# Two seven-product unit pairs moved from the fourth and sixth to the second and fourth place of an up panel pair

## The chip, the cores and the metric

The kernel runs on one core of a Trainium2 chip, as one launch. The metric is the device time of one execution in microseconds. A core has a matrix engine (TensorE, in the profile PE, with its weight loads as PEld), a vector engine (VectorE, DVE), a scalar engine (ScalarE, ACT), GpSimd (POOL) and SyncE (SP). The engines run their own instruction streams in order and wait for each other through semaphores. In this kernel SP issues the loads of the weights; ACT issues the transfers that turn tiles through DRAM.

## What is computed

Two layers of a decoder trunk on 256 tokens of width 2048 in float32: a gated linear attention layer and a forgetting attention layer, each with attention into 256 memory tokens, and each followed by a gated channel mixer. The change touches the first product of the mixer, `h @ w_up`:

```python
def conv_ffn(h, w_up, conv_w, conv_b, w_down):       # w_up: 2048 x 11264, w_down: 5632 x 2048
    u = causal_dwconv(h @ w_up, conv_w, conv_b)      # width 3, along the tokens
    a, val = split_cols(u, [FFN_HIDDEN, FFN_HIDDEN])
    return (jax.nn.silu(a) * val) @ w_down
```

## The kernel before

**Products in three parts.** A float32 product is made of three matmuls in a rounded format (float32r): the operands are cut into a high and a low part, and high x high, low x high and high x low are added in PSUM. The activations `h` are cut once (`split`). The weights are cut as they arrive: a unit of 128 x 1024 is loaded into `raw` (five buffers), ACT casts it to `whi`, and VectorE subtracts to get `wlo` (four buffers each). In `split_unit` these are lines 210, 211 and 220.

**Panels and units.** A weight panel of 512 columns and 2048 rows is eight units (`count` = 8), each with two chunks of 128 rows. `proj_tm` goes through one panel, `proj_two` through two with the activations of both 128-token halves. For the mixer, the 5632 hidden columns are worked through in three parts (`PARTS`: 16, 16 and 12 blocks of 128). An up panel holds two blocks of the gate and the same two of the value. Part one has eight up panels: two by `proj_two`, then two panel pairs by `seven_evacuated`, then two by `proj_tm`. Part two has three panel pairs and two single panels, part three two and two. After the up panels of a part come its four down panels. That makes seven panel pairs for each layer, and fourteen in all.

**Seven products in place of eight.** `proj_seven` takes two panels at once. For each of the eight places `u` there is a unit of the one and a unit of the other panel, a unit pair. At most places it makes the usual 24 matmuls (2 panels x 2 token halves x 2 chunks x 3 parts). At the places in `forms` it takes the 2 x 2 blocks of weights and tokens and makes seven block products in place of eight (21 matmuls). It pays for that with sums: `t13` and `t24` are sums of weight blocks (four VectorE subtractions of 128 x 512, lines 349 to 352), and these are cut as well (`halves`, lines 317 and 318: three of 128 x 1024 and one of 128 x 512, against two of 128 x 1024 at a plain place). The sums of the activations are made once for each mixer into the `mixed` tiles. Of the seven products three add straight into accumulators `acc`, and four have PSUM banks of their own (`m1`, `m5`, `m6`, `m7`; tiles `ps_t`, `ps_s` and `ps_o`). After the last place in `forms` the function `more` of `seven_evacuated` adds these up (lines 384 to 388) into the buffers of `t13` and `t24`, of which there is one each. There they stay, as `extra`, until the panels are evacuated after the eighth place: ACT scales an accumulator into `scaled` (line 1172), VectorE adds `extra` (line 1174) and transposes (line 442). The down panels (`add_seven`) use the same function with places three and five, or three, five and seven, counted from zero; their `more` (lines 1055 to 1062) runs after the last place.

**What sets the order.** The instructions are written out in program order, and a planner reorders them by priority and by its own simulated times. The loads and cuts of the weights get a priority as though they stood 300 instructions earlier (`AHEAD`), the subtractions for `t13` and `t24` 340. The order on each engine is fixed when the kernel is built. Other steps hang on a counter: `later((n, step))` runs a step after `n` more calls of `passed`, and every unit pair calls it twice, so a panel pair counts sixteen. An up panel writes its transposed tile at count 3, reads it back at 6, and is convolved at 8 to 11 (its partner at 10 to 13), in units of the panels that follow. The two sums for `mixed` are called at counts 18 and 20 from the mixer's start. Sixteen counts belong to `proj_two`, so both fall into the first panel pair.

Of the kernel before, what the change touches and what calls it, by code (L numbers as in the profile page):

```python
# [38 lines left out]
AHEAD = 300  # L39
SEVEN = ((3, 5), (3, 5, 7))  # L40
LAST = ()
UP = (3, 5)

SPREAD = [128 * q + 32 * k + i for k in range(4) for i in range(32) for q in range(4)]

# [95 lines left out]
def _trunk(ctx: ExitStack, tc: tile.TileContext, xt, xtok, memt, wp, wgu, gns, gfin, cnv, par, msk, out):  # L141
# [39 lines left out]
    def later(*steps):  # L181

        for units, step in steps:
            due.append([units, step])
# [190 lines left out]
    def seven_evacuated(keys, src, forms, evacs, tiles):  # L375

        n = where[keys[0]][0][2]
        extra = {}

        def more(m1, m5, m6, m7):  # L380
            p, q = (tiles(t, F32) for t in ("t13", "t24"))
            u, v, w = p[:, :n], p[:, n : 2 * n], q[:, :n]
            m1, m5, m6, m7 = (m[:, :n] for m in (m1, m5, m6, m7))
            S.activation(u, m1, AF.Copy)
            V.tensor_tensor(u, u, m6, ALU.add)
            V.tensor_tensor(v, u, m5, ALU.add)
            V.tensor_tensor(u, u, m7, ALU.add)
            V.tensor_tensor(w, u, m5, ALU.add)
            extra.update({(0, 0): m1, (1, 0): v, (0, 1): u, (1, 1): w})

        def evac(i):
            return lambda b, a: evacs[i](b, a, extra[i, b])

        proj_seven(keys, src, forms, [evac(i) for i in range(2)], tiles, more, True)

    def sums_of(src, chunks, f, h, form):

        for c, k in enumerate(chunks):
            V.tensor_tensor(h[:, c, :], *(src[k][:, i, :].bitcast(F32) for i in range(2)), ALU.add)
        (a0, a1), (b0, b1) = ([h[:, c, b * P : (b + 1) * P] for b in range(2)] for c in range(2))  # L400
        token_sums(a0, a1, b0, b1, f, form)
# [665 lines left out]
    def ffn(l, nx, h, m, then, ending=None):  # L1067
        with tc.tile_pool(name=f"ffn{l}", bufs=1) as fp, ExitStack() as ends:
# [16 lines left out]
            def form(t):  # L1085
                return lambda i: [t[:, k, i, :] for k in range(2)]

            mixed = [sp.tile([P, 2, 4, P], F32R, name=f"mixed{i}") for i in range(len(UP))]

            def mixed_at(u, t):  # L1090
                def step():
                    f, g = (tp.tile([P, 512], F32, name=n, tag="scaled", bufs=2) for n in ("sf", "sh"))
                    sums_of(h, (2 * u, 2 * u + 1), f.rearrange("p (i t) -> p i t", t=P),
                            g.rearrange("p (c t) -> p c t", t=T), [t[:, k, :, :] for k in range(2)])

                return step

            later(*[(18 + 2 * i, mixed_at(u, t)) for i, (u, t) in enumerate(zip(UP, mixed))])

            def taps(t, u, j, n, c):  # L1100

# [63 lines left out]
            def panel(j, base, slack=0):  # L1165
                held = []

                def evac(b, a, extra=None):
                    if not held:
                        held.append(Turn("turned"))  # L1170
                    e = tp.tile([P, 512], F32, name="scaled", tag="scaled", bufs=2)
                    S.activation(e, a, AF.Copy, scale=nx.col()[:, b : b + 1])
                    if extra is not None:
                        V.scalar_tensor_tensor(e, extra, nx.col()[:, b : b + 1], e, ALU.mult, ALU.add)
                    held[0].put(b, e)
                    if not b:
                        return
                    u = us[turn[0] % 2]
                    turn[0] += 1
                    later((3, held[0].write), (6, lambda: held[0].read(lambda k: u[:, k, 2:])))  # L1180
                    convolved(j, base, u, 8 + slack, j + 2 in (p[1] for p in PARTS))

                return evac

            parts = {lo: dict(zip(SEVEN[1] if p < len(PARTS) - 1 else LAST, tiles)) for p, (lo, _) in enumerate(PARTS)}
            for p, (lo, hi) in enumerate(PARTS):
# [5 lines left out]
                while len(js) > 2:  # L1192
                    seven_evacuated([("up", l, j) for j in js[:2]], h, {u: form(t) for u, t in zip(UP, mixed)},
                                    [panel(js[0], lo), panel(js[1], lo, 2)], spare_tile)
# [42 lines left out]
    memory[0].close()  # L1237
    n2, then, turns = preparing("kv", bufB)
    ffn(0, n, bufB, bufA, then)
    n, then, _ = preparing("ffn1", bufA)  # L1240
    fox(n2, turns, then)
# [40 lines left out]
    def closing(ends):  # L1282
        op = ends.enter_context(tc.tile_pool(name="store", bufs=1))
        made["y"] = op.tile([P, 2, 512], F32, name="y")
        return op

    ffn(1, n, bufA, bufB, None, (opened, closing))


# [83 lines left out]
```

## Time and profile before

| | |
|---|---|
| median of 3 runs | 2232.72 us (2230.32 to 2238.43) |
| the profiled execution | 2234.48 us, of which the span from the first to the last instruction is 2232.7 us |
| granted TensorE clock | 0.998 |
| busy | PE 2214.0 us, DVE 1808.7, ACT 1448.6, POOL 44.7 |
| read from HBM | 470.44 MB |

The page of the profile gives the busy time of each engine, the chain of work that ended last, and groups of instructions by line of the kernel. A row such as `wlo<-raw,whi` names what an instruction writes and reads. In a timeline, the bracket at the end of a row is the idle time of that engine ahead of the instruction, and what ended it. Up panel pairs of the first layer lie at about 508 to 594, 721 to 853 and 980 to 1065 us of the span, those of the second at about 1553 to 1638, 1767 to 1898 and 2024 to 2111.

### The profile page before, as it was taken

The page shows a single profiled execution, that of the slowest core. Times are in us where ns is not written, and L with a number is a line of the kernel's source. Part 1 is how long each engine was busy: PE and PEld are TensorE (multiplying, and loading weights), DVE is VectorE, ACT ScalarE, POOL GpSimd, SP SyncE. Part 2 cuts the span into 40 slices and gives each one's busy share as a digit, 9 for nine tenths or more (in the row PEclk, how much of TensorE's full clock was granted, in tenths as well). Part 3 has the DMA queues.
Part 4 walks back from the last instruction along what each step waited for, and adds up shares of the span by engine and source line. Part 5 has one row for each costly group of instructions (what it writes and reads, how often), then busy time and mean ns, then how long its engine had stood idle before and what let it go on. Part 6 is the DMA issues. An engine that isn't in the chain of part 4 may idle for free.

```text
span 2232.7 us, 29804 instructions
## 1 busy us (share of the span) xinstructions
PE 2214.0 (99%) x10183; PEld 1846.8 (83%) x10183; DVE 1808.7 (81%) x2650; ACT 1448.6 (65%) x2261; POOL 44.7 (2%) x71
## 2 busy tenths in 40 slices
PE   9999999999999999999999999999999999999998
PEld 7888888888888878888888898888888887888876
DVE  8568987669999898998877875666989989898876
ACT  7555666557785588657866555555877567855774
POOL 0000000000000000000000000000000000000000
PEclk9999999999999999999999999999999999999999
DMA  9875667677876678667878777668776667766684
GB/s 346 272 234 187 210 204 225 204 238 231 258 235 208 228 225 257 220 203 234 262 245 277 249 224 232 195 224 262 235 248 232 198 226 227 262 217 206 228 252 144
DMA packets 276896, 517.00 MB, mean 232 GB/s; under 512 B 149884, under 2 KB 158600, under 8 KB 276616
## 3 DMA queue, kind: packets, MB, share of 16 engines
q1 hardware_dynamic: 124296, 427.24, 57.7%
q10 hardware_dynamic: 149760, 80.51, 12.5%
q0 software_dynamic: 2688, 7.34, 1.2%
q8 instruction: 80, 1.31, 0.2%
q14 instruction: 72, 0.59, 0.1%
HBM read 470.44 MB, written 44.58 MB: 231 GB/s over the span
## 4 chain that ended last, share of the span: by engine, by line
PE 92%; DVE 2%; ACT 2%; DMA 2%; issue 1%; ACTq 0%; SPq 0%; DVEq 0%
PE acc L294 36%; PE acc L232 16%; PE acc L233 16%; PE acc L236 16%; PE ps_s L294 3%; PE ps_o L294 2%; PE ps_t L294 1%; DMA raw<-wp 1%; DMA turned<-square 1%; DVE wlo L220 1%; ACT whi L211 1%; ACT back L1109 1%; PE ps_s L837 0%; DVE wlo L318 0%; ACT back L1107 0%
## 5 line engine op out<-in xcount | busy, mean ns | idle before, releaser
L220 DVE TENSOR_TENSOR wlo<-raw,whi 128x1024 fp32r<-128x1024 f32 (+4 forms) x707 | 839.7, 1195 | 260.9 <-ACT whi L211 220.0
L211 ACT ACTIVATE whi<-raw 128x1024 fp32r<-128x1024 f32 (+4 forms) x707 | 725.2, 1035 | 427.6 <-PE acc L233 204.9
L232 PE MATMUL acc<-whi,B 128*128 128x512 f32 (+3 forms) x992 | 373.6, 381 | 1.3 <-ACT whi L211 1.3
L233 PE MATMUL acc<-whi,B 128*128 128x512 f32 (+3 forms) x992 | 373.3, 379 | 0.0
L294 PE MATMUL acc<-whi,B 128*128 128x512 f32 x1236 | 324.7, 392 | 2.1 <-ACT whi L211 2.1
L294 PE MATMUL acc<-whi,A 128*128 128x512 f32 x1224 | 321.6, 390 | 2.9 <-ACT whi L211 2.9
L294 PEld LDWEIGHTS acc<-whi,B 128*128 128x128 f32 x1236 | 232.8, 189 | 52.2 <-ACT whi L211 2.7
L294 PEld LDWEIGHTS acc<-whi,A 128*128 128x128 f32 x1224 | 229.5, 188 | 52.6 <-ACT whi L211 4.0
L232 PE MATMUL acc<-whi,A 128*128 128x512 f32 x672 | 261.3, 394 | 0.3 <-ACT whi L211 0.2
L233 PE MATMUL acc<-whi,A 128*128 128x512 f32 x672 | 260.3, 391 | 0.0
L236 PE MATMUL acc<-wlo,B 128*128 128x512 f32 (+3 forms) x992 | 257.0, 377 | 0.0
L232 PEld LDWEIGHTS acc<-whi,B 128*128 128x128 f32 x992 | 186.2, 188 | 31.1 <-ACT whi L211 1.7
L233 PEld LDWEIGHTS acc<-whi,B 128*128 128x128 f32 x992 | 186.0, 188 | 29.1 <-DVE B L528 0.4
L236 PEld LDWEIGHTS acc<-wlo,B 128*128 128x128 f32 x992 | 183.7, 188 | 28.7
L236 PE MATMUL acc<-wlo,A 128*128 128x512 f32 x672 | 182.2, 390 | 0.0
L294 PE MATMUL acc<-wlo,B 128*128 128x512 f32 x618 | 174.4, 390 | 0.0
L294 PE MATMUL acc<-wlo,A 128*128 128x512 f32 x612 | 173.6, 390 | 0.0
L318 DVE TENSOR_TENSOR wlo<-t,whi 128x1024 fp32r<-128x1024 f32 x102 | 123.8, 1221 | 35.1 <-ACT whi L317 27.8
L317 ACT ACTIVATE whi<-t 128x1024 fp32r<-128x1024 f32 x102 | 106.8, 1054 | 66.3 <-PE acc L294 44.2
L232 PEld LDWEIGHTS acc<-whi,A 128*128 128x128 f32 x672 | 126.2, 188 | 27.9 <-ACT whi L211 0.9
L233 PEld LDWEIGHTS acc<-whi,A 128*128 128x128 f32 x672 | 126.3, 188 | 26.1 <-DVE A L531 0.2
L236 PEld LDWEIGHTS acc<-wlo,A 128*128 128x128 f32 x672 | 126.0, 188 | 26.4 <-DVE wlo L220 0.3
(278 smaller groups left out, 2594.4 us busy)
## 6 DMA issues: line engine op xcount, KB each, us to landing
raw<-wp SPq DMA_DIRECT2D x743, 512.0 KB, 4.4
turned<-square ACTq DMA_DIRECT2D x61, 512.0 KB, 4.5
u<-turned ACTq DMA_DIRECT2D x176, 128.0 KB, 4.4
raw<-wp SPq DMA_DIRECT2D x32, 384.0 KB, 3.2
raw<-wp SPq DMA_DIRECT2D x24, 388.0 KB, 5.3
xturned<-square ACTq DMA_DIRECT2D x12, 512.0 KB, 4.2
back<-xturned ACTq DMA_DIRECT2D x40, 128.0 KB, 5.1
raw<-wp SPq DMA_DIRECT2D x8, 400.0 KB, 3.3
```

The costliest lines, as they stand in the source:

```text
L211: casts.append(S.activation(hi[:, s], raw[:, s], AF.Copy))
L220: V.tensor_tensor(lo[:, s], raw[:, s], hi[:, s].bitcast(F32), ALU.subtract)
L232: TE.matmul(acc[:, :n], xh, hi[:, s], start=first and j == 0, stop=False)
L233: TE.matmul(acc[:, :n], xl, hi[:, s], start=False, stop=False)
L236: TE.matmul(a, xh, ls, start=False, stop=stop)
L294: TE.matmul(a[:, :n], x, w, start=k not in begun, stop=calls[k] == 0)
L317: casts.append(S.activation(hi, raw, AF.Copy))
L318: V.tensor_tensor(lo, raw, hi.bitcast(F32), ALU.subtract)
L1109: S.activation(t[:, k, :], u[:, k, n : T + n], AF.Copy, scale=g[n])
```

## The change

The two places in `UP`, counted from zero, become 1 and 3 in place of 3 and 5. The weights are taken in the same order as before, and the number of instructions of each kind in a panel pair is the same. As the activation sums belong to the chunks of these places, they are now made of chunks 2, 3, 6 and 7 (before: 6, 7, 10 and 11), and the steps that make them are called at counts 10 and 12, which is within `proj_two`.

```diff
-UP = (3, 5)
+UP = (1, 3)
...
-            later(*[(18 + 2 * i, mixed_at(u, t)) for i, (u, t) in enumerate(zip(UP, mixed))])
+            later(*[(10 + 2 * i, mixed_at(u, t)) for i, (u, t) in enumerate(zip(UP, mixed))])
```

## The prediction

> **What bounds the kernel now.** I read the page first (engine totals, then the chain that ended last), then the windows cut at the fourteen pairs of up panels that the edit touches, then the timelines of VectorE (DVE), ScalarE (ACT) and TensorE (PE) around the two windows that stood out.
>
> ```profile
> PE 2214.0 (99%) x10183; PEld 1846.8 (83%) x10183; DVE 1808.7 (81%) x2650; ACT 1448.6 (65%) x2261; POOL 44.7 (2%) x71
> ...
> PE 92%; DVE 2%; ACT 2%; DMA 2%; issue 1%; ACTq 0%; SPq 0%; DVEq 0%
> ```
>
> TensorE sets the time: 2214.0 of 2232.7 us busy and 92% of the chain. The edit keeps every matmul, so it can only move the 18.7 us in which PE is idle, and what a stall costs in clock. The windows show how little of that lies in the fourteen pairs (columns: length, busy time of PE, PEld, DVE, ACT and POOL, granted clock, DMA share, GB/s).
>
> ```profile
> 720.60:763.00 42.40, 42.40 (x187) 34.92 (x186) 36.96 (x43) 22.60 (x25) 0.00 (x0) 1.00 0.66 215
> 763.00:805.30 42.30, 42.30 (x187) 34.84 (x187) 37.16 (x45) 33.10 (x52) 0.00 (x0) 1.00 0.70 228
> 805.30:853.00 47.70, 45.60 (x193) 36.83 (x192) 44.05 (x54) 35.95 (x57) 0.00 (x0) 0.96 0.75 237
> 1851.00:1898.00 47.00, 44.07 (x192) 35.67 (x191) 41.81 (x51) 34.43 (x56) 0.00 (x0) 1.00 0.73 229
> sum 607.00, PE 601.83 PEld 493.80 DVE 544.06 ACT 432.11 POOL 0.00; mean PE 42.99 PEld 35.27 DVE 38.86 ACT 30.86 POOL 0.00
> ```
>
> A pair takes some 42.3 us, PE all of it, except in two windows, one for each layer: the third pair of the middle part. Over all fourteen PE idles 607.00 - 601.83 = 5.17 us, of which 2.10 and 2.93 lie there; the clock of 0.96 costs the first another 0.04 x 47.7 = 1.9 us. So 7.1 us is all that the touched code could give back.
>
> What makes those two stalls: VectorE, cut into quarters of the pair before the first of them.
>
> ```profile
> 763.00:773.60 10.60, 10.60 (x48) 8.77 (x48) 10.60 (x15) 5.69 (x8) 0.00 (x0) 1.00 0.56 187
> 773.60:784.20 10.60, 10.60 (x49) 8.74 (x48) 5.46 (x7) 6.76 (x11) 0.00 (x0) 1.00 0.84 293
> 784.20:794.80 10.60, 10.60 (x48) 8.71 (x47) 10.60 (x13) 10.21 (x17) 0.00 (x0) 1.00 0.75 213
> 794.80:805.40 10.60, 10.60 (x49) 8.68 (x48) 10.60 (x13) 10.43 (x18) 0.00 (x0) 1.00 0.65 220
> ```
>
> VectorE is full while it evacuates the pair before (first quarter), half idle in the second, then full to the end, where both seven-product pairs, the convolution and the sums `more` fall together. What that leads to, from the chain (two rows), ACT (three) and PE (one):
>
> ```profile
> 807.78 1.15 DVE wlo L220
> ...
> 808.94 4.59 DMA raw<-wp
> ...
> 809.55 0.76 ACT L527 ACTIVATE A<-back 128x256 fp32r<-128x256 f32 x2 [0.73 <-DVE back L1139]
> 813.55 0.63 ACT L317 ACTIVATE vhi<-raw 128x512 fp32r<-128x512 f32 x1 [3.25 <-DMA raw<-wp]
> ...
> 814.09 1.04 ACT L211 ACTIVATE whi<-raw 128x1024 fp32r<-128x1024 f32 x1
> ...
> 815.18 4.11 PE L294 MATMUL acc<-whi,B 128*128 128x512 f32 x10 [2.10 <-ACT whi L211]
> ```
>
> The late subtraction at 807.78 frees a `raw` buffer late; the load into it starts at 808.94 and takes 4.59 us; ACT stands 3.25 us at the cast `vhi` of the coming seven-product pair; behind it in ACT's order waits the plain cast `whi` for which PE stands 2.10 us. The other layer has the same shape:
>
> ```profile
> 1858.87 0.63 ACT L317 ACTIVATE vhi<-raw 128x512 fp32r<-128x512 f32 x1 [3.28 <-DMA raw<-wp]
> ...
> 1860.50 3.01 PE L294 MATMUL acc<-whi,A 128*128 128x512 f32 x12 [1.91 <-ACT whi L211]
> ```
>
> **The change part by part.** Nothing is added or removed; three things move.
>
> (1) *The seven-product pairs leave the end of the panel pair.* VectorE's durations:
>
> ```profile
> L220 DVE TENSOR_TENSOR wlo<-raw,whi 128x1024 fp32r<-128x1024 f32 x11 | 13.0, 1216 | 1.5 <-ACT whi L211 1.5
> L318 DVE TENSOR_TENSOR wlo<-t,whi 128x1024 fp32r<-128x1024 f32 x4 | 4.9, 1222 | 5.1 <-ACT whi L317 5.1
> L442 DVE STREAM_TRANSPOSE square<-scaled 128x512 f32<-128x512 f32 x4 | 2.8, 704 | 0.0
> L318 DVE TENSOR_TENSOR vlo<-raw,vhi 128x512 fp32r<-128x512 f32 x2 | 1.4, 690 | 0.0
> L349 DVE TENSOR_TENSOR t<-raw 128x512 f32<-128x512 f32 x2 | 1.4, 684 | 0.0
> L1174 DVE SCALAR_TENSOR_TENSOR scaled<-ps_t,ny,scaled 128x512 f32<-128x512 f32 x1 | 0.7, 745 | 0.0
> ```
>
> A plain unit pair costs VectorE 2 x 1.22 = 2.4 us against 5.44 us of PE (24 matmuls at 42.3/187 = 0.226 us). A seven-product one costs four `t` subtractions, one `vlo` and three full ones, 4 x 0.68 + 0.69 + 3 x 1.22 = 7.1 us, against 21 x 0.226 = 4.75 us. The new places put 14.2 us of it into the first half of the panel pair in place of the second. The convolution (due from the third unit pair on) and `more` then meet only plain unit pairs. The backlog at the end of the second pair should go, the `raw` buffer come free in time, and the two stalls that the late load made with them: 2.10 + 1.9 + 1.91 = 5.9 us off. The rest of the second window, 2.93 - 1.91 = 1.02 us, has another cause, and I leave it in. Ends for this term: 0 and -7.1; I take -5.9, since both rows name one cause.
>
> (2) *The first seven-product pair comes one plain unit pair after the panel pair's start, not three.* `t13` and `t24` have one buffer each, and hold what the evacuation of the pair before adds (`extra`). So the next `t` can be formed only after that evacuation. How long this takes today, in the pair that begins at 763.0:
>
> ```profile
> 768.65 0.68 DVE L349 TENSOR_TENSOR t<-raw 128x512 f32<-128x512 f32 x1
> ...
> 770.48 0.71 DVE L1174 SCALAR_TENSOR_TENSOR scaled<-t,ny,scaled 128x512 f32<-128x512 f32 x1
> ...
> 774.61 0.65 DVE L352 TENSOR_TENSOR t<-raw,t 128x512 f32<-128x512 f32 x1
> ```
>
> The last `t` is done at 775.3, 12.3 us into the pair, at no cost, since PE needs it only past 763 + 3 x 5.44 = 779.3. In the new order PE comes to the first seven-product pair after 5.44 us and to its last low part 19 matmuls later: 5.44 + 19 x 0.226 = 9.7 us. VectorE no longer has to do the second plain unit pair in that time (-2.4), which puts the last `t` at 9.9 us; its cast and low part add two passes of 1.1 to 1.2 us: 12.2 us, or 2.5 us late. Whether that stops PE depends on the order written for it. It does run plain products between those of a seven-product pair today:
>
> ```profile
> 580.64 1.09 PE L294 MATMUL ps_s<-whi,mixed 128*128 128x512 f32 x4
> ...
> 582.97 2.44 PE L294 MATMUL acc<-whi,B 128*128 128x512 f32 x10
> ...
> 586.17 0.40 PE L294 MATMUL ps_o<-wlo,mixed 128*128 128x512 f32 x1
> ```
>
> With the next plain unit pair run in between, PE has 5.44 us more, for which VectorE pays 2.4 us: late by 2.5 + 2.4 - 5.44, that is, by nothing, with 0.5 us to spare. Ends: 0 and 2.5 us for each of the eight pairs that follow another seven-product panel pair. I take 0.7, nearer to 0, since these rows show PE's order leaving such room, but not 0: VectorE has little slack in a pair with all of this work (44.05 of 47.70 us busy in the window from 805.30). 8 x 0.7 = +5.6 us. The casts of ACT (3.5 for a seven-product pair, two for a plain one) move along and are covered by ACT's idle time (5.69 of 10.6 us busy in the first quarter); the loads for them go to SP earlier and cost nothing while `raw` comes free.
>
> Four pairs follow down panels. There the evacuation is four additions and the seven of `more`:
>
> ```profile
> 717.84 0.69 DVE L1039 TENSOR_TENSOR x<-x,acc 128x512 f32<-128x512 f32 x1 [0.74 <-PE acc L294]
> ...
> 734.68 1.21 DVE L1062 TENSOR_TENSOR x<-x,ps_s 128x1024 f32<-128x1024 f32 x1
> ...
> 722.49 1.07 PE L294 MATMUL acc<-whi,B 128*128 128x512 f32 x4
> ```
>
> They run from 717.84 to 735.9 today, between high-priority splits, while PE starts the up panels at 722.49 and idles nowhere (42.40 of 42.40). The work alone is 10 x 0.68 + 1.21 = 8.0 us; with unit pair 0 (2.4) and the first seven-product pair (7.1) VectorE would finish at 717.84 + 17.5 = 735.3, against 722.49 + 9.7 = 732.2 in strict order and 737.6 with a plain unit pair between (for 2.4 more: 737.7). Ends 0 and 3.1; I take 1.0, again nearer to the filled order: 4 x 1.0 = +4.0 us.
>
> (3) *The two sums for the `mixed` weights move into the two-panel stretch ahead of the first pair* (steps 10 and 12 instead of 18 and 20).
>
> ```profile
> L399 DVE TENSOR_TENSOR sh<-B x6: 417/419/421, 515.2 to 1180.0; 128x256 f32<-128x256 f32 x6
> L410 DVE TENSOR_TENSOR mixed<-sf,mixed x4: 679/682/687, 524.8 to 1581.6; 128x512 fp32r<-128x512 f32 x4
> ...
> 490.00:500.00 10.00, 10.00 (x46) 8.29 (x45) 4.12 (x4) 4.24 (x4) 0.00 (x0) 1.00 0.59 184
> ```
>
> Each is about 2 x 0.42 + 4 x 0.28 (shorter ones of 128) + 0.68 = 2.6 us of VectorE and one short cast. The end of that stretch has VectorE at 4.12 of 10 us, and the steps issue no DMA, so this is hidden; without that cover it would be 2.6 us twice per layer. The first pair itself gets 5.3 us of room for its earlier seven-product pair, and its predecessor leaves no `extra`. I count 0 for both layers, ends -0.5 and +2.5.
>
> Sum: -5.9 + 5.6 + 4.0 = +3.7 us. On the profiled execution's own 2234.48 us that is 2238.2; that execution lies 1.8 us above the median of 2232.72, from which the same sum gives 2236.4.
>
> **The rivals.** About 0.5% (11 us) is what a measurement of this kernel can tell from no change; the three runs shown spread by 8 us.
>
> *A, slower: the evacuation holds the first seven-product pair, and PE stands.* For it: `t` formed only at 12.3 us in the rows above, one buffer each. Against it: the plain products between. If PE's order doesn't give way, 8 x 2.5 + 4 x 3.1 - 5.9 = +26 us: 2259. It decides (over +11 us) from (11 + 5.9)/12 = 1.4 us for each of the twelve pairs. A price hangs on it that the two stalls show:
>
> ```profile
> 816.00:818.00 2.00, 2.00 (x6) 1.52 (x6) 2.00 (x3) 1.23 (x2) 0.00 (x0) 0.50 0.28 100
> 1861.00:1863.00 2.00, 2.00 (x10) 1.63 (x10) 2.00 (x3) 1.90 (x4) 0.00 (x0) 1.00 0.45 152
> ```
>
> After 2.10 us of idling the clock fell to 0.50; after 1.91 us it did not. So a stall of 2 us or more may cost twice itself, and A could reach 2259 + 8 x 1.9 = 2274. [...]
>
> *B: only the gain.* All of part 2 is filled: -5.9 us, 2226.8. For it: 12 of the 14 windows idle for 0.14 us together today (5.17 - 2.10 - 2.93), so PE's order has met such chains well. Against it: VectorE's first quarter is full already.
>
> *C: the two stalls stay.* The load is late for another reason than VectorE's backlog, and part 2 is paid: 2232.7 + 9.6 = 2242.3. For it: ACT stands at the same `vhi` cast in both layers. Against it: the row of 807.78 ends right before the load.
>
> *D, faster by over 11 us.* The pairs hold only 7.1 us; it needs stalls elsewhere to go as well.
>
> **How the numbers follow.** My forecast 0.36, A 0.28, B 0.22, C 0.10, D 0.04. So faster 0.04, within 0.5% 0.68, slower 0.28. The forecast's own range is 2229 to 2243; with B below and the nearer half of A above, 2225 to 2256.
>
> **What would show it.** Right: no idle and clock 1.00 in the third pair of the middle parts, and VectorE's busy time highest in the first half of a pair, with idle time in the last quarter. Part 2: PE waits of 0.5 to 1.5 us at `acc` or `ps_s` with `whi` or `wlo` of L317/L318 before them, 5 to 15 us after a pair's start. Wrong: such waits near 2.5 us in every pair with clock rows of 0.5 (A), none (B), a `vhi` cast still behind a late `raw` (C).

## The result and the profile after

The changed kernel takes 2239.81 us (median of 20 runs) against 2232.66 us (20 runs): 1.0026 of the kernel before, with a 95% interval of 1.0017 to 1.0035. By the medians that is 7.1 us slower, by the means 5.8, to which the ratio is closer; either lies within half a per cent. The forecast was +3.7 us.

The same views after, the page first, then the windows at the fourteen pairs, moved by the few microseconds that each pair starts later (two rows and the sum):

```profile
PE 2216.9 (99%) x10183; PEld 1845.5 (82%) x10183; DVE 1810.6 (81%) x2650; ACT 1448.2 (65%) x2261; POOL 44.7 (2%) x71
```

```profile
807.10:855.00 47.90, 45.34 (x193) 36.71 (x192) 43.60 (x52) 37.42 (x61) 0.00 (x0) 0.96 0.73 225
...
1855.50:1903.00 47.50, 44.78 (x194) 35.76 (x194) 42.84 (x52) 36.69 (x59) 0.00 (x0) 1.00 0.73 223
...
sum 607.20, PE 599.76 PEld 488.00 DVE 537.62 ACT 418.42 POOL 0.00; mean PE 42.84 PEld 34.86 DVE 38.40 ACT 29.89 POOL 0.00
```

Work and matmuls are the same; PE idles for 7.44 us in the pairs where it idled for 5.17, and the third pair of the middle part is still the worst, in both layers. The cause there is a new one. VectorE, ACT and PE at its start, first layer (timelines):

```profile
806.62 1.22 DVE L1127 TENSOR_TENSOR back<-back 128x1024 f32<-128x1024 f32 x1
...
810.84 1.19 DVE L1127 TENSOR_TENSOR back<-back 128x1024 f32<-128x1024 f32 x1
...
813.19 0.69 DVE L1139 TENSOR_TENSOR back<-back 128x512 f32<-128x512 f32 x1
...
815.63 0.71 DVE L1174 SCALAR_TENSOR_TENSOR scaled<-t,ny,scaled 128x512 f32<-128x512 f32 x1
816.25 0.76 DVE L528 TENSOR_TENSOR A<-back,A 128x256 fp32r<-128x256 f32 x2
816.92 1.22 DVE L318 TENSOR_TENSOR wlo<-t,whi 128x1024 fp32r<-128x1024 f32 x1
818.06 0.69 DVE L351 TENSOR_TENSOR t<-raw,t 128x512 f32<-128x512 f32 x1
...
819.29 0.65 DVE L352 TENSOR_TENSOR t<-raw,t 128x512 f32<-128x512 f32 x1
...
820.04 1.06 ACT L317 ACTIVATE whi<-t 128x1024 fp32r<-128x1024 f32 x1 [3.85 <-DVE t L352]
...
818.20 0.73 PE L294 MATMUL ps_s<-wlo,mixed 128*128 128x512 f32 x2 [0.34 <-DVE wlo L318]
821.14 0.79 PE L294 MATMUL ps_o<-whi,mixed 128*128 128x512 f32 x1 [2.22 <-ACT whi L317]
```

The last evacuation (L1174, 815.63) frees the buffer, L351 and L352 form `t24`, ACT casts it, and PE has stood 2.22 us for that cast. VectorE itself is idle nowhere from 806.62 to 819.94: a rest of the convolution (L1127 twice, L1139 and L528, 3.86 us together) and a low part (816.92) stand among these steps. So the hold and a full VectorE are both in this chain, and its rows alone can't part them. No row at `vhi` waits for a load there any more.

VectorE over the pair ahead of it, in quarters:

```profile
764.80:775.40 10.60, 10.60 (x48) 8.63 (x46) 9.37 (x14) 3.81 (x6) 0.00 (x0) 1.00 0.45 157
775.40:786.00 10.60, 10.60 (x47) 8.46 (x46) 9.19 (x11) 7.99 (x12) 0.00 (x0) 1.00 1.06 294
786.00:796.60 10.60, 10.60 (x49) 8.71 (x48) 10.41 (x11) 9.96 (x16) 0.00 (x0) 1.00 0.71 239
796.60:807.20 10.60, 10.60 (x48) 8.79 (x47) 9.15 (x12) 9.20 (x16) 0.00 (x0) 1.00 0.85 286
```

The hole of the kernel before (5.46 of 10.60 us in its second quarter) is filled and the load is nearly even, highest in the third quarter. But the convolution isn't done when the next pair starts, at about 807.1: L1127, L1139 and L528 still run up to 817.01.

For the sums below I took the start of the same matmul, by its number in PE's order, at the bounds of each stage, in every profile, and subtracted the first profile of the kernel before. Microseconds:

| stage | before, again | after | after, again | e1 | e2 | e3 | e4 | e5 | e6 | e7 | e9 | e10 | e12 |
|---|---|---|---|---|---|---|---|---|---|---|---|---|---|
| 2 pairs after `proj_two` | 0.0 | 0.0 | 0.0 | -0.1 | 3.8 | 0.0 | 0.0 | 0.0 | 0.0 | 0.0 | 0.4 | 0.0 | 0.0 |
| 4 pairs after down panels | 0.0 | 3.2 | 3.7 | 0.0 | 6.8 | 2.8 | 0.0 | 0.1 | 1.8 | -0.3 | 0.0 | 4.6 | 0.1 |
| 2 third pairs of the middle part | -2.5 | 0.3 | 3.6 | -3.9 | 1.7 | -4.4 | -4.2 | -3.0 | 2.0 | -1.2 | -1.4 | -4.3 | -4.0 |
| 6 other second pairs | 2.9 | 2.0 | 1.4 | 1.0 | 4.1 | 1.7 | 1.8 | 3.1 | 3.8 | 7.3 | 0.5 | 1.7 | 3.0 |
| all else | -0.9 | -0.1 | -1.8 | 3.7 | 2.3 | 6.1 | -1.7 | 2.4 | 5.6 | 1.8 | 11.6 | 0.2 | 1.3 |
| span | -0.5 | 5.4 | 6.8 | 0.8 | 18.7 | 6.2 | -4.1 | 2.5 | 13.2 | 7.6 | 11.1 | 2.3 | 0.3 |

Each column is one execution: those of e6 and e9 took 4.1 and 4.6 us more than the median of their runs, those of e7 and e10 6.1 and 4.8 us less.

### The profile page after: what moved, and what is told of

It is laid out like the page before. It is cut to its first block, busy times and chain, and to the rows that moved or that the text cites. A ratio compares the mean times of both kernels' runs of the same rounds, so it can differ in the third digit from the quotient of the medians.

```text
span 2238.1 us, 29781 instructions
## 1 busy us (share of the span) xinstructions
PE 2216.9 (99%) x10183; PEld 1845.5 (82%) x10183; DVE 1810.6 (81%) x2650; ACT 1448.2 (65%) x2261; POOL 44.7 (2%) x71
## 4 chain that ended last, share of the span: by engine, by line
PE 92%; DVE 3%; DMA 3%; ACT 1%; issue 1%; SPq 0%; ACTq 0%; DVEq 0%
PE acc L294 36%; PE acc L232 16%; PE acc L233 16%; PE acc L236 16%; PE ps_s L294 3%; PE ps_o L294 2%; PE ps_t L294 1%; DMA raw<-wp 1%; DMA back<-turned 1%; DVE wlo L220 1%; DVE wlo L318 0%; DMA xturned<-square 0%; DMA back<-xturned 0%; PE ps_s L837 0%; DVE scaled L1174 0%
## 5 line engine op out<-in xcount | busy, mean ns | idle before, releaser
L317 ACT ACTIVATE whi<-t 128x1024 fp32r<-128x1024 f32 x102 | 107.8, 1059 | 127.4 <-DVE t L352 53.4
L318 DVE TENSOR_TENSOR wlo<-t,whi 128x1024 fp32r<-128x1024 f32 x102 | 124.1, 1223 | 26.8 <-ACT whi L317 24.3
```

What stands on the lines that cost most here:

```text
L317: casts.append(S.activation(hi, raw, AF.Copy))
L318: V.tensor_tensor(lo, raw, hi.bitcast(F32), ALU.subtract)
```

## The experiments

The profile of after left one theory, "chain" (the evacuation, through the single buffers of `t13` and `t24`, holds the first seven-product pair), and three against it: the moved sums, a VectorE that is full in any order, and a planner whose every new order makes stalls somewhere. The ratios below are to runs of the kernel before made beside each experiment, whose median was 2235.96 us for e1 to e4, 2234.39 for e5 to e7 and 2236.06 for e9, e10 and e12.

### e1 and e2: the two halves of the edit

```diff
 UP = (3, 5)          # e1: only the sums move
-later(*[(18 + 2 * i, ...
+later(*[(10 + 2 * i, ...
```
```diff
-UP = (3, 5)          # e2: only the places move, sums at 18 and 20
+UP = (1, 3)
```

> The places stay the fourth and sixth; only the two activation sums are called at counts 10 and 12 instead of 18 and 20. Theory 'chain' (the new stalls come from t13/t24 being held by the evacuation of the pair before, so that the first seven-product pair, one plain pair later, waits): the sums cost little, 2231 to 2235 us against 2232.7 before, and the 4 us stall at the third pair of part two stays with its old cause (a late raw load). Theory 'sums' (the sums disturb the two-panel stretch and the first pair; the changed kernel has a new 1.7 us stall at 1508 us, ahead of the first pair): 2236 to 2240 us.

> The places are the second and fourth, with the sums left at counts 18 and 20 (now in the first panel pair, just ahead of their use). Theory 'chain': 2237 to 2242 us, with PE waits of 2.4 us at ps_o behind the cast of t24 in the third pair of part two, as in the changed kernel (2239.8). Theory 'sums': back to 2231 to 2235. If the sums are now too late for the first pair, a further wait of 1 to 3 us in each layer's first pair.

e1: 2237.26 us, 1.0003 of before (0.999 to 1.0016). e2: 2253.58 us, 1.007 (1.0051 to 1.0088). The median of e1 lies in the range of "sums", but the kernel before was slower in these runs too: by the ratio the sums alone cost nothing that can be told, so they are not what made the change slower. The stall of the third pairs stays in e1, as "chain" said, behind a late `raw` (ACT stands 3.12 and 2.96 us at `vhi`, PE 1.80 and 0.55). The places alone cost more than the whole change, and more than either theory said: the sums have to move with them. The first pair of each layer is longer, by 1.5 and 2.3 us, as the last sentence expected of sums that come too late. The wait of 2.2 us at `ps_o` in the third pair is there again, as is a longer wait after down panels (PE, both from e2):

```profile
824.22 0.57 PE L294 MATMUL ps_o<-whi,mixed 128*128 128x512 f32 x1 [2.21 <-ACT whi L317]
...
1792.35 1.20 PE L294 MATMUL acc<-whi,A 128*128 128x512 f32 x4 [1.80 <-ACT whi L211]
```

Why e2 loses time in pairs that the sums don't touch is open. e1 has a stall of its own, in down panels that it doesn't touch either:

```profile
902.28 3.28 PE L294 MATMUL acc<-whi,A 128*128 128x512 f32 x8 [2.12 <-ACT whi L211]
```

### e3 and e4: no hold on t13 and t24

```diff
-            p, q = (tiles(t, F32) for t in ("t13", "t24"))
-            u, v, w = p[:, :n], p[:, n : 2 * n], q[:, :n]
+            u, v, w = (tiles(t, F32)[:, :n] for t in ("e01", "e10", "e11"))
```

> The changed kernel, but the sums that the evacuation adds (extra) get three tiles of their own instead of the buffers of t13 and t24; no work is added or removed. Theory 'chain': the subtractions for t13 and t24 no longer wait for the evacuation, the PE waits at ps_o and ps_s behind casts of t (about 9 us over the fourteen pairs, clock loss with them) go, and the time falls to 2229 to 2233 us. Theory 'full VectorE' (the first half of a pair has more VectorE work than fits, whatever its order): the waits move to acc or whi and the time stays at 2236 to 2241.

> The kernel before with the same three tiles of its own for extra. Theory 'chain': at the fourth place the hold is covered by two more plain pairs, so nothing much changes, 2229 to 2235 us, and the stall at the third pair of part two stays, since it comes from the late raw load. Theory 'full VectorE': no change either, 2231 to 2235. If it gains as much as the changed kernel does from the same edit, the hold was no matter of the places.

e3 (new places): 2241.54 us, 1.0018 (1.0005 to 1.0031). e4 (old places): 2233.41 us, 0.9983 (0.9972 to 0.9994), below the kernel before (2235.96) and the fastest here by its ratio. The function edited also serves two pairs of attention projections in the second layer, so the edit reaches those as well. In e3 the wait of 2.2 us at `ps_o` in the third pairs is gone; at 815.40 PE stands 0.55 us in its place (first row), and later in that pair 0.65 us at another `ps_o` and 0.44 at `acc`:

```profile
815.40 0.73 PE L294 MATMUL ps_s<-wlo,mixed 128*128 128x512 f32 x2 [0.55 <-DVE wlo L318]
...
1721.04 0.50 PE L294 MATMUL ps_o<-whi,forms 128*128 128x512 f32 x1 [1.43 <-ACT whi L317]
```

So the hold makes that wait. But the time can't be told from that of the changed kernel (1.0026). The table shows where the gain went: the fourteen pairs of e3 are level with before (0.1 us together), and 6.1 us appeared elsewhere, the largest parts in down panels, such as the 1.43 us of the second row; the changed kernel stands there for 0.26 us. Nothing in the down panels was edited. "Chain" names the wait rightly and its prediction of the time fell; "full VectorE" has the time, but not the place where it went.

Between the old and the new places the same tiles leave a difference of 8.1 us by the medians (e3 less e4), where the kernels with the hold differ by 7.1. So the hold is shown to make the wait, and not shown to make the time: with it gone the places cost as much, in other stages. By the time alone, the last sentence expected of e4 came true, since the old places gained no less from the tiles. In the trace its gain is another: ACT still stands 3.15 and 2.99 us at `vhi`, PE behind it 2.02 and 0.90, and what is gone is part of PE's waits (2.10 and 1.91 us before).

### e5 and e12: one place later

```diff
-UP = (1, 3)
+UP = (2, 4)          # e12: with the three tiles of e3 besides
```

> The places are the third and fifth (2, 4 from zero), sums at counts 10 and 12. Theory 'chain' (the evacuation of the pair before, through t13 and t24, reaches the first seven-product pair): there is one more plain pair, 5.4 us, ahead of it, so the waits of 2.4 us at ps_o in the third pair of part two shrink below 0.5; and the late raw load of the kernel before is eased too: 2229 to 2235 us. Theory 'planner' (any new order makes new stalls of a few us somewhere, whatever the place): the fourteen pairs give back what the single and down panels lose, 2235 to 2241.

> Places three and five (2, 4 from zero), sums at counts 10 and 12, and three tiles of its own for extra. Theory 'chain': the hold no longer matters and VectorE's load is spread more evenly than at the old places: PE waits in the fourteen pairs under 4 us together, 2229 to 2234 us, about as the kernel before with tiles of its own (0.9983 of before). Theory 'planner': what the pairs gain comes back in the down panels, 2234 to 2239.

e5: 2236.28 us, 1.0013 (1.0001 to 1.0025). e12: 2233.08 us, 0.9992 (0.9977 to 1.0007). With one plain pair more, the four pairs after down panels cost 0.1 us where places 1 and 3 cost 3.2 and 3.7: that term belongs to the first place. The wait at `ps_o` in the third pair of e5 is 1.04 us in both layers, over the 0.5 expected. The pairs as a whole are level with before, and what is left of the loss lies in down panels. e12, which has no hold, still shows 2.06 us at `ps_o` in the first layer's third pair (834.85), in front of its second seven-product pair: ACT, which casts `t24`, comes to it only after the transfers and products of `u`. So a wait at `ps_o` is not by itself a sign of the hold. The ratios lie closer to 1 than the theories' times allow to choose by.

### e6: the evacuation ahead in priority

```diff
+with tc.high_priority(offset=0 if extra is None else AHEAD + 60):
     S.activation(e, a, ...); V.scalar_tensor_tensor(e, extra, ...); held[0].put(b, e)
```

> The changed kernel, with the evacuation of a pair (scale, add extra, transpose) given a priority of 360 instructions, above the subtractions for t13 and t24, so that what is left of the convolution no longer stands ahead of it on VectorE. Theory 'chain': the last t of the third pair comes 3 us sooner, and its PE wait of 2.4 us at ps_o falls below 0.7, clock loss gone: 2231 to 2236 us. Theory 'full VectorE': the work ahead of it only changes places, PE waits at other operands in the same pair, 2237 to 2242.

2243.77 us, 1.004 (1.0025 to 1.0056). PE in the third pair stands three times, 2.66 us in all where the changed kernel stood 2.56 and 2.99:

```profile
818.68 1.19 PE L294 MATMUL ps_s<-whi,mixed 128*128 128x512 f32 x4 [0.93 <-ACT whi L317]
820.60 0.74 PE L294 MATMUL ps_s<-wlo,mixed 128*128 128x512 f32 x2 [0.72 <-DVE wlo L318]
822.34 0.69 PE L294 MATMUL ps_o<-whi,mixed 128*128 128x512 f32 x1 [1.01 <-ACT whi L317]
```

The convolution's instructions still stand between the evacuations in VectorE's order, so the edit didn't bring about what it was to test. That the rest of the convolution makes the third pair worse than other second pairs is argued and not shown: in the six others of the changed kernel none of its rows stands among the evacuations and the steps of `t`, but no run took it away from the third.

### e7 and e8: the old stall

```diff
-raw = wpool.tile([P, NUNIT], F32, name="raw", tag="raw", bufs=RING["raw"])[:, :w]
+raw = tiles("r1", F32)[:, :w]        # second unit of a seven-product pair only, places (3, 5)
```

> The kernel before, but the second raw unit of each seven-product pair is loaded into a tile of its own and not into the ring of five raw buffers; the work is the same. Theory 'late raw' (the old stall of the third pair of part two comes from a ring buffer freed late): the waits of ACT at vhi (3.25 and 3.28 us) and of PE (2.10 and 1.91 us) there go, with the clock loss in the first layer: 2227 to 2232 us. Theory 'full VectorE': PE waits there for another operand about as long, 2232 to 2237.

> The kernel before once more, unchanged, for a second profile. If the 1.3 us wait of PE at 2169 us, which the changed kernel and all variants so far lack, belongs to this order, it stands here again; if it was one late transfer in one execution, it is gone, and the change has 2 us less to its credit. The third pair of part two should show its 2 us wait in both layers again.

e7: 2248.19 us, 1.0054 (1.0036 to 1.0071). The waits at `vhi` in the third pairs went, as "late raw" said, but ACT now stands 5.67 us there for the read-back of `u`, and PE 0.37 and 1.01 us (two rows); in the second layer PE stands 1.64 and 0.20 us, nearly as long as before, as "full VectorE" said:

```profile
824.90 0.60 ACT L1110 ACTIVATE back<-u,cw 128x256 f32<-128x256 f32 x1 [5.67 <-DMA u<-turned]
```

```profile
831.55 2.13 PE L294 MATMUL acc<-whi,B 128*128 128x512 f32 x8 [0.37 <-ACT whi L211]
834.70 1.65 PE L294 MATMUL acc<-whi,B 128*128 128x512 f32 x6 [1.01 <-ACT whi L211]
```

The table has 7.3 us of its loss in the six other second pairs. Its new tile has one buffer and serves other seven-product pairs too, the down panels among them, so it may hold work of its own; why it is so much slower is open. e8 took 2234.05 us, with the same program as before, and its stall at that place is another:

```profile
811.75 0.63 ACT L317 ACTIVATE vhi<-raw 128x512 fp32r<-128x512 f32 x1 [2.55 <-DMA raw<-wp]
```

```profile
813.38 3.06 PE L294 MATMUL acc<-whi,B 128*128 128x512 f32 x12 [0.33 <-ACT whi L211]
832.21 2.11 PE L294 MATMUL acc<-whi,B 128*128 128x512 f32 x8 [0.94 <-ACT whi L211]
```

The wait for the late load belongs to this order, but its size doesn't: a load that came 1.8 us sooner left PE 0.33 us in place of 2.10, and the same execution paid 2.9 us in other second pairs. The wait at 2169 us of the first profile is gone. ACT stood there for one transfer (`turned`) ahead of its cast: from its issue to the next step took 5.29 us in the first profile and 4.19 in this one.

### e9 and e10: the additions left out; e11: the changed kernel again

```diff
-if extra is not None:
-    V.scalar_tensor_tensor(e, extra, nx.col()[:, b : b + 1], e, ALU.mult, ALU.add)
```

> The kernel before without the four additions of extra at line 1174 (left out in all fourteen pairs; the up panels miss that part of their result). That takes 4 x 0.66 us of VectorE from the start of each following pair or panel, and t13 and t24 are held by nothing there. At the fourth place the additions are off the path, but VectorE's backlog shrinks by 2.6 us for each pair: 2226 to 2231 us. Theory 'planner': 2230 to 2238.

> The changed kernel with the same four additions left out. Theory 'chain' (the cost of the new places is that the evacuation meets the first seven-product pair): with no additions and no hold the new places cost nothing more, and this lies within 3 us of the kernel before without the additions, with no PE wait over 0.7 us at ps_o 5 to 15 us after a pair's start. Theory 'sums and planner' (the cost lies outside of the pairs, in the stretch ahead of the first pair and in down panels): it stays 5 to 8 us above that kernel.

> The changed kernel once more, unchanged, for a second profile. Theory 'chain': the waits at ps_o in the third pairs of part two are set by VectorE's order and come again within 0.1 us (2.4 us in both layers), while waits on transfers, such as the 1.7 us at 1508 us, change from one execution to the next. If the waits at ps_o vary by a microsecond too, they depend on transfers as well.

e9: 2241.04 us, 1.0027 (1.0011 to 1.0043). e10: 2241.8 us, 1.0027 (1.0012 to 1.0042). Without the additions the two places cost the same, within 0.8 us of medians, and e10 has no wait at `ps_o` in any pair, as "chain" said. That is at odds with e3 and e4, where the hold was gone as well and the places still cost 8.1 us. In e10 the third pairs are 4.3 us under before, and only the pairs after down panels, whose evacuation was left whole, still pay 4.6 us. That each is slower than the kernel before, with 56 instructions less on VectorE, was expected by nobody: e9 loses it in down panels, where ACT stands for `u` and PE behind it (ACT, then PE):

```profile
662.92 0.60 ACT L1149 ACTIVATE back<-u,cw 128x256 f32<-128x256 f32 x1 [2.54 <-DMA u<-turned]
663.42 1.04 ACT L211 ACTIVATE whi<-raw 128x1024 fp32r<-128x1024 f32 x1
...
664.51 1.65 PE L294 MATMUL acc<-whi,A 128*128 128x512 f32 x6 [2.15 <-ACT whi L211]
```

e11 took 2241.26 us. The waits at `ps_o` come back to a hundredth (first layer, then second):

```profile
821.18 0.79 PE L294 MATMUL ps_o<-whi,mixed 128*128 128x512 f32 x1 [2.21 <-ACT whi L317]
...
1871.19 0.50 PE L294 MATMUL ps_o<-whi,mixed 128*128 128x512 f32 x1 [2.21 <-ACT whi L317]
```

The wait at 1508 us, behind another such transfer, shrank from 1.51 us to 0.32. The transfer took as long in both (5.64 and 5.74 us); PE came to it 1.4 us later in the second. So some of what that execution had lost before was won back here, and stages are not independent of each other.

## Why the prediction was right, and where it was not

The time came out slower and inside the range, and the bound held: PE sets the time, its work didn't change, and the effect lies in the fourteen pairs. The mean of the two profiles after, less that of the two before, gives +6.8 us there and -0.5 us for all else. Of the 6.8 us, 2.2 are idle time of PE (5.17 and 5.69 us before, 7.44 and 7.83 after) and some 2.6 are half-speed clock (the granted clock was 0.96 in one pair and 1.00 in all others before, 1.00 in all in its second profile, 0.96 in one pair after, 0.93 and 0.96 in two in its second profile); the rest shows as later starts without an idle row. Which terms made it is another matter.

- *Pairs after down panels:* forecast +4.0, measured +3.4. Right in place and total; e5 and e12 show that it hangs on the first place. But the forecast had 1.0 us for each, and they cost 0.05 to 2.4. Nor does PE stand where it was to (at the casts and low parts of L317 and L318): in the third part of the second layer, the costliest, it stands for an addition of the down panels' evacuation, which comes late, and for a plain cast. No run took that evacuation away.

```profile
2034.27 1.20 PE L294 MATMUL acc<-whi,A 128*128 128x512 f32 x4 [0.47 <-DVE x L1039]
2042.43 1.20 PE L294 MATMUL acc<-whi,A 128*128 128x512 f32 x4 [0.77 <-ACT whi L211]
```

- *The two old stalls, -5.9, and 0.7 for each second pair, +5.6:* this is where the sum failed. For the third pairs it makes -5.9 + 1.4 = -4.5; measured +3.2. The late load's wait went as forecast, but the evacuation put 2.2 us and a slow clock (0.50 for 3.41 us in the first layer) in its place, about the 2.5 us that I had worked out for a PE that finds nothing to fill with, where I took 0.7. The step that failed is the time of the last `t`. I had it 9.9 us into the pair; in the third pair it was done at 819.94, 12.8 us in, because the convolution that "meets only plain unit pairs" ran on into this pair. In the pair ahead, where no convolution stands among these steps, it was done 9.6 us after the start at 764.8, and PE idled nowhere (42.30 of 42.30 us):

```profile
773.71 0.68 DVE L352 TENSOR_TENSOR t<-raw,t 128x512 f32<-128x512 f32 x1
```

  The -5.9 was also too large, since it rested on one execution. The late load makes ACT stand 2.55 to 3.28 us at `vhi` in before, e8, e1 and e4 alike, but PE behind it 2.10, 0.33, 1.80 and 2.02 us in the first layer and 1.91, 1.53, 0.55 and 0.90 in the second, and of the four stalls of before and e8 only the first was followed by a half-speed clock (0.50 from 816 to 818 us; the windows of the other three pairs have 1.00).
- *The other six second pairs:* forecast 6 x 0.7 = +4.2, measured +0.2. So the third pairs came out 7.7 us above their part of the sum and these 4.0 below theirs. That the total is only 3.4 us off is in part luck.
- *The sums, 0:* e1 agrees. But that they are hidden at 10 and 12 doesn't mean that they could have stayed: e2 costs 0.70%.
- *The rivals:* A's mechanism came true in two pairs of twelve, not in all. B and D fell. C fell too: the late load's wait did go.
- *The signs:* the third pairs kept their idle time (2.56 and 2.72 us), and VectorE was busiest in the third quarter of the pair shown, with no idle last quarter.

## What to carry to other kernels

When a step that was late by design is made early, look for a single buffer that links it to the end of the round before: here `t13` and `t24` carried one round's result and the next round's input, and a tile of its own took that wait away, though not the time. In a kernel at 99% of one engine, a stall seen in one execution is not a term to subtract: profile the same program twice, and take only what comes back. And with an order made by a planner, an edit's own stage can come out as worked out while 2 to 11 us appear in a stage that nobody touched, so compare stage by stage before giving a time a cause.

## What the runs showed of the hardware

The same wait of PE had two prices. After 2.21 us of idling in the second layer's third pair, the clock stayed at 1.00 in one execution of the changed kernel (first row) and fell to 0.50 in the other (second row):

```profile
1871.00:1873.00 2.00, 2.00 (x10) 1.61 (x9) 1.19 (x3) 2.00 (x4) 0.00 (x0) 1.00 1.01 404
```

```profile
1872.00:1874.00 2.00, 2.00 (x6) 1.55 (x5) 1.06 (x3) 2.00 (x4) 0.00 (x0) 0.50 0.99 371
```

So the length of a wait does not decide it. The traces keep the times at which the granted clock changed, and these say more. In the first profiles of the two kernels the times from change to change are 808.96, 3.41 and 1409.70 us before and 815.79, 3.41 and 1409.70 us after: 237, 1 and 413, and 239, 1 and 413 steps of 3.413 us. The stretch at half speed is one such step in both. I added up PE's idle time in each step, without the first and last 20 us of the span. The clock fell after the step with the most idling, 2.05 us before and 2.16 us after, and after no other; the next highest have 1.10 and 1.51 us. The 2.21 us of the first row are cut in two by the end of a step (0.73 and 1.48 us). Those of the second row ran from 1868.98 to 1871.19 us. The two microseconds from 1870 have a clock of 0.90 in that execution and those from 1872 have 0.50, so by my estimate the clock fell at about 1871.6, and the step of 3.413 us ahead of that holds the wait whole. In these rows, then, the fall goes with the idling within one step and not with the length of a wait.
